# Copying both channels of a pair with one instruction in an im2col kernel

## The chip, the cores and the metric

The kernel runs on one core of a Trainium2 chip. The metric is the device time of one execution in microseconds (us). All executions quoted are fast (none took over 1.5% more than the fastest of its kernel), and every comparison of times is between runs of the same rounds on the same chip. Traces are single executions, and those of different groups of runs come from different chips. The profile comes from one execution of each kernel; its span (89.6 us here) is shorter than the device time (91.4 us for that execution).

## The reference

Each 3 x 3 window of a 32 x 32 image becomes a column. There are 16 x 64 images (fp32); each gives 9 planes of 30 x 30, one for each position (i, j) in the window, so the output has nine planes for each input image:

```python
# ... (cut: the loop over the batch b, which sets col_idx to 0)
for i in range(h_out):
    for j in range(w_out):
        patch = x[b, :, i:i + kernel_size, j:j + kernel_size].copy()
        cols[b, :, col_idx] = patch.ravel()
        col_idx += 1
```

No arithmetic is done. 4.19 MB are read from device memory (HBM) and 33.18 MB are written.

## The kernel before

Each of the 128 partitions holds eight images ("channels" below), treated in four pairs. A first load brings pair 0, a second one the other three. VectorE and ScalarE copy a pair's 18 planes from the input tile to an output tile, and one DMA stores the tile. There are two output tiles, so pair 2 must wait until the store of pair 0 has given its buffer back.

```python
in_pool = ctx.enter_context(tc.tile_pool(name="in_pool", bufs=1))
out_pool = ctx.enter_context(tc.tile_pool(name="out_pool", bufs=2))
# ... (cut)
first = load(0, 2 * H)
load(2 * H, CPP * H)

def planes(c, ki, kj, n, step):
    w = in_tile[:, c, ki : ki + HO, kj : kj + WO]
    part, row, col = [list(d) for d in w.ap]
    return bass.AP(w.tensor, w.offset, [part, [step, n], row, col])

for c in range(0, CPP, 2):
    out_tile = out_pool.tile([P, 2, KK, HO, WO], x.dtype, name="out_tile")
    for s in range(2):
        o = out_tile[:, s]
        nc.scalar.copy(out=o[:, K : 2 * K], in_=planes(c + s, 1, 0, K, 1))
        for ki in (0, 2):
            nc.vector.tensor_copy(
                out=o[:, ki * K : ki * K + 2], in_=planes(c + s, ki, 0, 2, 1)
            )
        # ... (cut: planes 2 and 8. For s == 0 one VectorE copy of both,
        #      for s == 1 plane 2 on VectorE and plane 8 on ScalarE)
    nc.sync.dma_start(
        out=out_v[:, c : c + 2].rearrange("p c n -> p (c n)"),
        in_=out_tile.rearrange("p c kk i j -> p (c kk i j)"),
    )
```

Of the kernel before, what the change touches and what calls it, by code (L numbers as in the profile page):

```python
# [1 line left out]

# [3 lines left out]


def _im2col(ctx, tc, x, K, out):


    nc = tc.nc
    P = nc.NUM_PARTITIONS

    B, C, H, W = x.shape
    HO = H - K + 1
    WO = W - K + 1
    KK = K * K
    assert out.shape == (B, C * KK, HO * WO)
    CPP = B * C // P
    assert CPP * P == B * C and C % CPP == 0 and CPP % 2 == 0 and K == 3  # L20

    x_v = x.rearrange("b (cp c2) h w -> (b cp) (c2 h w)", c2=CPP)
    out_v = out.rearrange("b (cp c2 kk) n -> (b cp) c2 (kk n)", c2=CPP, kk=KK)

    in_pool = ctx.enter_context(tc.tile_pool(name="in_pool", bufs=1))
    out_pool = ctx.enter_context(tc.tile_pool(name="out_pool", bufs=2))

    ctx.enter_context(tc.manual_schedule())

    in_tile = in_pool.tile([P, CPP, H, W], x.dtype, name="in_tile")  # L30
    in_flat = in_tile.rearrange("p c h w -> p (c h w)")

    def load(r0, r1):

        return nc.sync.dma_start(
            out=in_flat[:, r0 * W : r1 * W],
            in_=x_v[:, r0 * W : r1 * W],
        )

    first = load(0, 2 * H)  # L40
    load(2 * H, CPP * H)

    def planes(c, ki, kj, n, step):

        w = in_tile[:, c, ki : ki + HO, kj : kj + WO]
        part, row, col = [list(d) for d in w.ap]
        return bass.AP(w.tensor, w.offset, [part, [step, n], row, col])

    for c in range(0, CPP, 2):
        out_tile = out_pool.tile([P, 2, KK, HO, WO], x.dtype, name="out_tile")  # L50


        for s in range(2):
            o = out_tile[:, s]
            nc.scalar.copy(out=o[:, K : 2 * K], in_=planes(c + s, 1, 0, K, 1))  # L55
            for ki in (0, 2):
                nc.vector.tensor_copy(  # L57
                    out=o[:, ki * K : ki * K + 2], in_=planes(c + s, ki, 0, 2, 1)
                )
            if s == 0:  # L60
                nc.vector.tensor_copy(  # L61
                    out=o[:, 2:KK:6], in_=planes(c + s, 0, 2, 2, 2 * W)
                )
            else:
                nc.vector.tensor_copy(  # L65
                    out=o[:, 2], in_=in_tile[:, c + s, 0:HO, 2 : 2 + WO]
                )
                nc.scalar.copy(  # L68
                    out=o[:, 8], in_=in_tile[:, c + s, 2 : 2 + HO, 2 : 2 + WO]
                )  # L70
        nc.sync.dma_start(  # L71
            out=out_v[:, c : c + 2].rearrange("p c n -> p (c n)"),
            in_=out_tile.rearrange("p c kk i j -> p (c kk i j)"),
        )
    return first


def kernel(
    tc: tile.TileContext,
    x: bass.AP,  # L80
    kernel_size: bass.AP,
    out: bass.AP,
):
    with ExitStack() as ctx:
        first = _im2col(ctx, tc, x, int(kernel_size), out)


    tc.close()
    tc.compile()  # L89
    blocks = tc.nc.main_func.blocks  # L90
    load = first.ins
    home = next(b for b in blocks if any(i.name == load.name for i in b.instructions))
    home.instructions = [i for i in home.instructions if i.name != load.name]
    head = list(blocks[0].instructions)
    at = next(
        k
        for k, i in enumerate(head)
        if i.engine == load.engine and type(i).__name__ == "InstDrain"
    )
    head.insert(at, load)  # L100
    blocks[0].instructions = head


# [1 line left out]
_INS = ['x', 'kernel_size']  # L105
_OUTS = [((16, 576, 900), 'float32')]

_NUMBERS = {'kernel_size': 3}


# [26 lines left out]
```

## Time and profile before

| what | value |
|---|---|
| device time, median of 3 runs | 91.12 us (91.10 to 91.21) |
| profiled span | 89.6 us |
| VectorE / ScalarE busy | 25% / 27% of the span |
| DMA queue, share of 16 engines' span | 97.2% |
| first store issued | 10.69 us |

Read the engines' shares against the queue's share first. A queue at 97% leaves 3% to be won by work that feeds it, and only from stretches in which it stands idle. The groups by shape (busy us, mean ns of one | idle before, releasers) give the price of each kind of copy. L57 and L61 copy 1800 elements each by different patterns and take the same time (1092 and 1090 ns), so neither pattern is slower than the other:

```profile
L55 ACT COPY out_tile<-in_tile 128x2700 f32<-128x2700 f32 x8 | 19.2, 2443 | 31.7 <-DMA out_dram<-out_tile 27.1 <-DMA in_tile<-in_x_dram 4.5
L57 DVE COPY out_tile<-in_tile 128x1800 f32<-128x1800 f32 x16 | 16.8, 1092 | 33.7 <-DMA out_dram<-out_tile 27.1 <-DMA in_tile<-in_x_dram 6.6
L61 DVE COPY out_tile<-in_tile 128x1800 f32<-128x1800 f32 x4 | 4.4, 1090 | 0.0
L68 ACT COPY out_tile<-in_tile 128x900 f32<-128x900 f32 x4 | 3.8, 938 | 0.0
L65 DVE COPY out_tile<-in_tile 128x900 f32<-128x900 f32 x4 | 2.5, 620 | 0.0
```

### The profile page before, as it was taken

What the parts mean: (1) busy time and instruction counts of PE and PEld (TensorE: products, weight loads), DVE (VectorE), ACT (ScalarE), POOL (GpSimd) and SP (SyncE); (2) the same over time, 40 slices, a digit from 0 to 9 for tenths busy, and PEclk for the clock granted to TensorE, in tenths of its full rate; (3) what the DMA queues carried; (4) which work ended last, traced back from release to release, by engine and by line L of the source; (5) the groups of instructions that cost most, each with busy time, mean ns of one, the idle gap of its engine ahead of it and who ended that gap; (6) DMA issues with size and microseconds to landing.
All of it is one profiled execution on the core that took longest, in us unless ns stands there. A gap on an engine that the chain in (4) does not pass through costs nothing.

```text
span 89.6 us, 96 instructions
## 1 busy us (share of the span) xinstructions
DVE 22.6 (25%) x24; ACT 23.8 (27%) x13; POOL 0.2 (0%) x4
## 2 busy tenths in 40 slices
DVE  0079759900000099500000399100000000000000
ACT  5079759900000099500000399100000000000000
POOL 0000000000000000000000000000000000000000
DMA  5989899999999999947999999999999982999990
GB/s 128 505 384 494 362 463 463 463 463 463 463 463 463 463 463 463 434 174 318 463 463 463 463 463 463 463 463 463 463 463 463 463 347 116 463 463 463 463 463 0
DMA packets 864, 37.37 MB, mean 417 GB/s; under 512 B 96, under 2 KB 96, under 8 KB 96
## 3 DMA queue, kind: packets, MB, share of 16 engines
q1 hardware_dynamic: 864, 37.37, 97.2%
HBM read 4.19 MB, written 33.18 MB: 417 GB/s over the span
## 4 chain that ended last, share of the span: by engine, by line
DMA 49%; DVE 12%; DVEq 1%; issue 0%; SPq 0%
DMA out_dram<-out_tile 36%; DMA in_tile<-in_x_dram 13%; DVE out_tile L57 8%; DVE out_tile L61 2%; DVE out_tile L65 1%; DVEq L89 1%; DVEq L57 0%; SPq L71 0%
## 5 line engine op out<-in xcount | busy, mean ns | idle before, releaser
L55 ACT COPY out_tile<-in_tile 128x2700 f32<-128x2700 f32 x8 | 19.2, 2443 | 31.7 <-DMA out_dram<-out_tile 27.1
L57 DVE COPY out_tile<-in_tile 128x1800 f32<-128x1800 f32 x16 | 16.8, 1092 | 33.7 <-DMA out_dram<-out_tile 27.1
L61 DVE COPY out_tile<-in_tile 128x1800 f32<-128x1800 f32 x4 | 4.4, 1090 | 0.0
L68 ACT COPY out_tile<-in_tile 128x900 f32<-128x900 f32 x4 | 3.8, 938 | 0.0
L65 DVE COPY out_tile<-in_tile 128x900 f32<-128x900 f32 x4 | 2.5, 620 | 0.0
L55 ACT ACT_TABLE_LOAD x1 | 1.3, 1283 | 0.8 <-PEq L118 0.8
L118 POOL MEMSET const-bfloat16-1.0<- 128x1 bf16 x1 | 0.1, 101 | 0.0
L118 POOL MEMSET const-uint8-127<- 128x1 uint8 x1 | 0.1, 101 | 0.0
L118 POOL MEMSET const-float32-0.0<- 128x1 f32 x1 | 0.1, 98 | 0.2 <-issue 0.2
L118 POOL MEMSET const-float32-1.0<- 128x1 f32 x1 | 0.1, 98 | 0.0
## 6 DMA issues: line engine op xcount, KB each, us to landing
out_dram<-out_tile SPq DMA_DIRECT2D x4, 8100.0 KB, 32.4
in_tile<-in_x_dram SPq DMA_DIRECT2D x1, 3072.0 KB, 11.4
in_tile<-in_x_dram SPq DMA_DIRECT2D x1, 1024.0 KB, 4.9
```

What stands on the lines that cost most here:

```text
L55: nc.scalar.copy(out=o[:, K : 2 * K], in_=planes(c + s, 1, 0, K, 1))
L57: nc.vector.tensor_copy(out=o[:, ki * K : ki * K + 2], in_=planes(c + s, ki, 0, 2, 1))
L61: nc.vector.tensor_copy(out=o[:, 2:KK:6], in_=planes(c + s, 0, 2, 2, 2 * W))
L65: nc.vector.tensor_copy(out=o[:, 2], in_=in_tile[:, c + s, 0:HO, 2 : 2 + WO])
L68: nc.scalar.copy(out=o[:, 8], in_=in_tile[:, c + s, 2 : 2 + HO, 2 : 2 + WO])
L89: tc.compile()
L118: nc = _bacc.Bacc("TRN2", target_bir_lowering=False, num_devices=1)
```

## The change

The intent is fewer instructions for the same bytes: a source pattern with one more dimension, the channel, lets one copy cover both channels. VectorE goes from six copies per pair to three, ScalarE from three to two. Which planes each engine copies stays the same in number (11 and 7).

```diff
-    def planes(c, ki, kj, n, step):
+    def windows(c, n, ki, kj, m):
-        w = in_tile[:, c, ki : ki + HO, kj : kj + WO]
-        part, row, col = [list(d) for d in w.ap]
-        return bass.AP(w.tensor, w.offset, [part, [step, n], row, col])
+        w = in_tile[:, c : c + n, ki : ki + HO, kj : kj + WO]
+        part, chan, row, col = [list(d) for d in w.ap]
+        return bass.AP(w.tensor, w.offset, [part, chan, [1, m], row, col])
 ... (cut: the copies of before, shown above, go out)
+        for on_act, s, n, ki, kj, m in (
+            (True, 0, 2, 1, 0, K),
+            (False, 0, 2, 0, 0, K),
+            (False, 0, 2, 2, 0, 2),
+            (False, 0, 1, 2, 2, 1),
+            (True, 1, 1, 2, 2, 1),
+        ):
+            src = windows(c + s, n, ki, kj, m)
+            dst = out_tile[:, s : s + n, ki * K + kj : ki * K + kj + m]
+            if on_act:
+                nc.scalar.copy(out=dst, in_=src)
             else:
 ... (cut)
+                nc.vector.tensor_copy(out=dst, in_=src)
```

More of the change, by code (lines that the diff above doesn't have):

```diff
@@ L41, in _im2col @@
     load(2 * H, CPP * H)
-    def planes(c, ki, kj, n, step):
-        w = in_tile[:, c, ki : ki + HO, kj : kj + WO]
-        part, row, col = [list(d) for d in w.ap]
-        return bass.AP(w.tensor, w.offset, [part, [step, n], row, col])
+    def windows(c, n, ki, kj, m):
+        w = in_tile[:, c : c + n, ki : ki + HO, kj : kj + WO]
+        part, chan, row, col = [list(d) for d in w.ap]
+        return bass.AP(w.tensor, w.offset, [part, chan, [1, m], row, col])
     for c in range(0, CPP, 2):
         out_tile = out_pool.tile([P, 2, KK, HO, WO], x.dtype, name="out_tile")
-        for s in range(2):
-            o = out_tile[:, s]
-            nc.scalar.copy(out=o[:, K : 2 * K], in_=planes(c + s, 1, 0, K, 1))
-            for ki in (0, 2):
-                nc.vector.tensor_copy(
-                    out=o[:, ki * K : ki * K + 2], in_=planes(c + s, ki, 0, 2, 1)
-                )
-            if s == 0:
-                nc.vector.tensor_copy(
-                    out=o[:, 2:KK:6], in_=planes(c + s, 0, 2, 2, 2 * W)
-                )
-            else:
-                nc.vector.tensor_copy(
-                    out=o[:, 2], in_=in_tile[:, c + s, 0:HO, 2 : 2 + WO]
-                )
-                nc.scalar.copy(
-                    out=o[:, 8], in_=in_tile[:, c + s, 2 : 2 + HO, 2 : 2 + WO]
-                )
+        for on_act, s, n, ki, kj, m in (
[9 more added lines that the diff above has]
+                nc.scalar.copy(out=dst, in_=src)
+            else:
+                nc.vector.tensor_copy(out=dst, in_=src)
         nc.sync.dma_start(
```

## The prediction

Passages for which no trace or run of this case stands are cut from the text, and the cuts are marked. The forecast's sum is 91.12 − 0.06 = 91.06 us. Of the rates, 0.522 ns per element is VectorE's and 0.836 ScalarE's; that the new copies would run at them was an estimate. Rival 1 supposes that VectorE needs twice its measured time per element (1.044 ns) for the large copies, whose patterns have four dimensions (2 channels, 3 or 2 planes, 30 rows, 30 columns). Rival 3 supposes that they take a quarter longer (a guess, also the "small collision" of the range) because what one copy reads and writes lies farther apart: 4,096 and 32,400 bytes from channel to channel, where L57 has 4 and 3,600 from plane to plane.

> **What bounds the kernel now.** I read the page first, parts 1 and 3: which engine is busy, and how busy the transfer queue is.
>
> ```profile
> DVE 22.6 (25%) x24; ACT 23.8 (27%) x13; POOL 0.2 (0%) x4
> ...
> q1 hardware_dynamic: 864, 37.37, 97.2%
> ```
>
> VectorE and ScalarE each work for a quarter of the 89.6 us span; packets of the one DMA queue fill 97.2% of 16 engines' span. So the copies matter only where the queue would otherwise stand idle. The chain of waits, second, tells where the copies lie beside transfers (start, us, what):
>
> ```profile
> 0.79 11.40 DMA in_tile<-in_x_dram
> ...
> 17.33 0.55 DVE out_tile L65
> ...
> 17.95 32.59 DMA out_dram<-out_tile
> ...
> 50.65 1.10 DVE out_tile L57
> ```
>
> It needs care. It follows the last engine instruction, so it stops at 56.3 us, and it shows a copy of pair 3 waiting for a store to give its buffer back. The reader might take those copies (12% of the span) for critical. They are not: the store of pair 1 lands at 50.5, but the store of pair 2 was issued at 37.25 (timeline of the issuing queue) and stands behind it, so the transfers go on while pair 3 is built. Landings, from issue plus time to landing, are 31.4, 50.5, 69.7 and 88.8: even steps of 19.1 us, which is 8,294,400 bytes at 434 GB/s. Only the first pair's copies lie ahead of any store. The timeline shows that stage (start, length, engine, line):
>
> ```profile
> 4.93 4.79 ACT L55 COPY out_tile<-in_tile 128x2700 f32<-128x2700 f32 x2 [2.87 <-DMA in_tile<-in_x_dram]
> 4.93 2.10 DVE L57 COPY out_tile<-in_tile 128x1800 f32<-128x1800 f32 x2 [4.93 <-DMA in_tile<-in_x_dram]
> 6.96 1.09 DVE L61 COPY out_tile<-in_tile 128x1800 f32<-128x1800 f32 x1
> 7.96 2.10 DVE L57 COPY out_tile<-in_tile 128x1800 f32<-128x1800 f32 x2
> 9.63 0.94 ACT L68 COPY out_tile<-in_tile 128x900 f32<-128x900 f32 x1
> 9.97 0.62 DVE L65 COPY out_tile<-in_tile 128x900 f32<-128x900 f32 x1
> 10.69 7.60 SPq L71 DMA_DIRECT2D out_dram<-out_tile  x2
> ```
>
> ScalarE ends at 10.57, VectorE at 10.59; the first store is issued at 10.69. Is the queue idle then? Windows of 0.1 us, which book a packet where it starts (last two columns: DMA share, GB/s):
>
> ```profile
> 10.00:10.10 0.10, 0.10 (x2) 0.10 (x1) 0.00 (x0) 1.00 0.57 246
> ...
> 10.90:11.00 0.10, 0.00 (x0) 0.00 (x0) 0.00 (x0) 1.00 0.57 246
> ...
> 11.50:11.60 0.10, 0.00 (x0) 0.00 (x0) 0.00 (x0) 1.00 15.20 6480
> 11.60:11.70 0.10, 0.00 (x0) 0.00 (x0) 0.00 (x0) 1.00 7.60 3240
> ...
> 11.80:11.90 0.10, 0.00 (x0) 0.00 (x0) 0.00 (x0) 1.00 1.50 648
> ```
>
> The sixteen last packets of the second load (24,576 bytes, 0.912 us each in the trace's packet records) start between 10.0 and 11.0; by those records they end from 11.24 to 11.83, fifteen of them by 11.56. The first packets of the store start from 11.54 to 11.84. So the first store's packets start 0.85 us after its issue, just as the load runs out. Some engines stand idle for up to 0.3 us. The last one goes from its load packet to its store packet in 2 ns.
>
> [...] by the groups of instructions VectorE's 1800 elements take 1090 ns and 900 take 620, a slope of 470/900 = 0.522 ns per element[...]. In both large new copies the outermost dimension is the channel, count 2, on both sides. [...] (2443 − 938)/1800 = 0.836 ns per element, 186 ns fixed, and two copies in 4.79 us overlap by 0.096. [...]
>
> **The change part by part.** The change's title counts eleven instructions before; the page counts nine per pair (24 copies of VectorE and 12 of ScalarE in four pairs). VectorE has six copies before (five of 1800, one of 900) and three after (5400, 3600, 900); ScalarE three before (2700, 2700, 900) and two after (5400, 900). The two loads, the stores, the buffers and the elements per engine (9,900 and 6,300) stay as they are. Both channels of a pair arrive in one load, so one instruction over both waits for nothing new.
> - VectorE. Before: five steps of (9.97 − 4.93)/5 = 1.008 us, then 0.62: 5.66 us, ending at 10.59. One copy overlaps the next by 1.090 − 1.008 = 0.082. After: the large ones are 150 + 0.522 × 5400 = 2970 ns and 150 + 0.522 × 3600 = 2030 ns. 2.97 − 0.08 + 2.03 − 0.08 + 0.62 = 5.46 us, ending at 10.39. Saving 0.20 us.
> - ScalarE. Before 4.79 + 0.94 less 0.09: 5.64 us, ending at 10.57. After: 186 + 0.836 × 5400 = 4700 ns; 4.70 − 0.10 + 0.94 = 5.54 us, ending at 10.47. Saving 0.10 us.
> - ScalarE now ends last. Issue follows at 10.47 + 0.10 = 10.57, which is 0.12 us earlier, and the first store packets could start at 11.42.
>
> What is on the path: only this 0.12 us of pair 0. The load itself still ends from 11.24 to 11.83. Five engines gain the full 0.12, ten gain 0 to 0.12 and the last gains nothing. As the store ends when its slowest engine ends, and the sixteen land within 0.18 us of each other, I expect 0.00 to 0.10 off the end and choose 0.06: about half[...]. In the three other pairs, the 0.12 us falls into time in which a store is in flight, with slack of 31.4 − 18.0 = 13 us for pair 1, 13 for pair 2 (37.25 against 50.5) and 13 for pair 3 (56.4 against 69.7). It is worth nothing there. Sum: 91.12 − 0.06 = 91.06 us.
>
> **The rivals.**
> 1. [...] the two large copies would cost 0.15 + 1.044 × 5.4 = 5.79 and 3.91 us; pair 0 would end at 4.93 + 5.79 + 3.91 − 0.16 + 0.62 = 15.09, and the store start 4.5 us later, with the queue empty: 95.6 us, 5% slower. The other pairs' 13 us of slack would hide it. For it: before, no copy has more than three such dimensions in its recorded pattern. Against: [...] the record's patterns have room for four.
> 2. *A new wait between the engines.* ScalarE writes planes 3 to 5 of both channels, VectorE planes 0 to 2 and 6 to 7 around them. If the dependences were kept by enclosing ranges, one engine would wait for the other, and pair 0 would take 5.5 + 5.4 us rather than 5.66: again some 96 us. Against: L61 before writes planes 2 and 8 as one stepped pattern, which encloses planes 3 to 5 of the same channel. It started at 6.96, with no idle time, while ScalarE's copy of those planes ran until 7.38. So the dependences saw between the steps there; I do not know that they do for the larger patterns.
> 3. [...] A quarter more time would make VectorE's large copies 1.25 us longer and cost some 1.1 us (92.2). Against: L61 reads 256 and writes 21,600 bytes apart and takes 1090 ns like L57.
> 4. *The whole 0.12 us comes through*[...]: 91.0. In the extreme this is still 0.13%.
>
> **Range and chances.** The three runs before spread over 0.11 us. From 0.12 us gained and a run's scatter below, and a scatter and small collision above: 90.9 to 91.35. Faster by 2% would need 1.8 us, fifteen times what the copies can give on the path: 0.01. Rivals 1 and 2 get 4% each, rival 3 near 1%: slower 0.08. The rest, 0.91, is within 2%.
>
> **What would show it.** VectorE's forms: 128x5400 near 2970 ns, 128x3600 near 2030, 128x900 at 620; ScalarE's: 5400 near 4700. In pair 0 ScalarE ends last, near 10.47, and the store is issued near 10.57; its first packets start near 11.42 and its last first packet still near 11.84. Landings keep steps of 19.1 us. A 5400 copy near 5800 ns is rival 1; idle time of one engine until the other within a pair is rival 2; 3000 to 3800 ns is rival 3. I am wrong if the time leaves 90.9 to 91.35, or if the copies are as told and the end moves by more than the first store's issue does.

## The result, and the profile after

| | before | changed |
|---|---|---|
| median of six runs | 91.19 us (91.10 to 91.30) | 91.28 us (91.16 to 91.42) |
| ratio of changed to before | | 1.001, 95% interval 0.9996 to 1.0024 |

A ratio is the mean time of one kernel's fast runs over that of the other's of the same rounds, so not quite the ratio of the medians. The time before is here the median of six runs, three of them those of the section above.

From the page of the changed kernel, the engines and the queue:

```profile
DVE 21.8 (24%) x12; ACT 23.5 (26%) x9; POOL 0.2 (0%) x4
...
q1 hardware_dynamic: 864, 37.37, 97.1%
```

The groups by shape:

```profile
L63 ACT COPY out_tile<-in_tile 128x5400 f32<-128x5400 f32 x4 | 18.8, 4701 | 31.9 <-DMA out_dram<-out_tile 27.3 <-DMA in_tile<-in_x_dram 4.7
L65 DVE COPY out_tile<-in_tile 128x5400 f32<-128x5400 f32 x4 | 11.9, 2974 | 34.3 <-DMA out_dram<-out_tile 27.5 <-DMA in_tile<-in_x_dram 6.8
L65 DVE COPY out_tile<-in_tile 128x3600 f32<-128x3600 f32 x4 | 8.1, 2029 | 0.0
L63 ACT COPY out_tile<-in_tile 128x900 f32<-128x900 f32 x4 | 3.8, 938 | 0.0
L65 DVE COPY out_tile<-in_tile 128x900 f32<-128x900 f32 x4 | 2.5, 623 | 0.0
```

Half as many VectorE instructions save 0.8 us of its busy time in the whole kernel. The copies after the first of a pair have no idle time before them, so no engine waits for the other inside a pair. The timeline of the first pair (several copies of one line are merged under the shape of the first):

```profile
4.95 5.54 ACT L63 COPY out_tile<-in_tile 128x5400 f32<-128x5400 f32 x2 [2.88 <-DMA in_tile<-in_x_dram]
4.95 5.45 DVE L65 COPY out_tile<-in_tile 128x5400 f32<-128x5400 f32 x3 [4.95 <-DMA in_tile<-in_x_dram]
10.52 0.35 SPq L66 DMA_DIRECT2D out_dram<-out_tile  x1
```

VectorE ends at 10.40 and ScalarE at 10.49; the store is issued at 10.52, which is 0.17 us earlier than before. Here are the windows at the junction of load and store, a packet booked where it starts (last two columns: DMA share, GB/s):

```profile
11.30:11.40 0.10, 0.00 (x0) 0.00 (x0) 0.00 (x0) 1.00 4.59 1944
11.40:11.50 0.10, 0.00 (x0) 0.00 (x0) 0.00 (x0) 1.00 13.64 5832
11.50:11.60 0.10, 0.00 (x0) 0.00 (x0) 0.00 (x0) 1.00 4.52 1944
...
11.80:11.90 0.10, 0.00 (x0) 0.00 (x0) 0.00 (x0) 1.00 1.50 648
```

Set them beside those of before: the bulk of the first store packets moves forward, but one packet still starts between 11.8 and 11.9, as before. By its time it belongs to the DMA engine whose load ends last: the packet records of the trace (start, length and size of every DMA packet) carry no engine number, but that store packet starts within 2 ns of the end of the last load packet. By these records the last store packet lands at 88.30 us, before at 88.33.

### The profile page after: what moved, and what is told of

Same layout as the page of the kernel before. It is cut to its first block, busy times and chain, and to the rows that moved or that the text cites. A ratio compares the mean times of both kernels' runs of the same rounds, so it can differ in the third digit from the quotient of the medians.

```text
span 89.6 us, 80 instructions
## 1 busy us (share of the span) xinstructions
DVE 21.8 (24%) x12; ACT 23.5 (26%) x9; POOL 0.2 (0%) x4
## 4 chain that ended last, share of the span: by engine, by line
DMA 49%; ACT 11%; ACTq 1%; issue 0%
DMA out_dram<-out_tile 36%; DMA in_tile<-in_x_dram 13%; ACT out_tile L63 11%; ACTq L84 1%; ACTq L63 0%
## 5 line engine op out<-in xcount | busy, mean ns | idle before, releaser
L63 ACT COPY out_tile<-in_tile 128x5400 f32<-128x5400 f32 (+1 forms) x8 | 22.2, 2819 | 31.9 <-DMA out_dram<-out_tile 27.3
L65 DVE COPY out_tile<-in_tile 128x5400 f32<-128x5400 f32 (+2 forms) x12 | 21.8, 1875 | 34.3 <-DMA out_dram<-out_tile 27.5
```

Source lines behind the costliest of these rows:

```text
L63: nc.scalar.copy(out=dst, in_=src)
L65: nc.vector.tensor_copy(out=dst, in_=src)
```

## The experiments

All kernels gave correct results. Diffs are against the changed kernel. "Jobs" stands for the list of tuples (engine is ScalarE, first channel, channels, row, column, planes).

**Each engine's part alone.** `e5_scalar_part` keeps the old VectorE copies, `e6_vector_part` the old ScalarE copies.

```diff
 e5_scalar_part, jobs (the copy at row 0, column 2 of two planes has its old stepped pattern)
-            (False, 0, 2, 0, 0, K), (False, 0, 2, 2, 0, 2), (False, 0, 1, 2, 2, 1),
+            (False, 0, 1, 0, 0, 2), (False, 0, 1, 2, 0, 2), (False, 0, 1, 0, 2, 2),
+            (False, 1, 1, 0, 0, 2), (False, 1, 1, 2, 0, 2), (False, 1, 1, 0, 2, 1),
 e6_vector_part, jobs
-            (True, 0, 2, 1, 0, K),
+            (True, 0, 1, 1, 0, K), (True, 1, 1, 1, 0, K),
```

> ScalarE's part of the change alone (5400 and 900); VectorE keeps its six copies. Only the later engine of pair 0 counts: VectorE ends 5.66 us after the start of the copies and the first store is issued 5.76 us after it, as before (10.69 - 4.93), nothing gained. If shorter ScalarE work alone moved the issue, 5.57 as with both parts. Time 91.3, the same.

> VectorE's part alone (5400, 3600, 900); ScalarE keeps its three copies. ScalarE ends 5.64 us after the start of the copies. If the issue comes 0.03 us after ScalarE where it is last and 0.10 after VectorE where that is last, as the two traces so far suggest, the store is issued 5.67 us after the start: half of the change's 0.19 us from VectorE's part alone, of which 0.07 is the shorter way from ScalarE's end to the issue. If that way is 0.10 whichever engine is last, 5.74. Time 91.3, the same; the end of the last store follows the last load packet by 76.5 us in both runs.

Times: 91.20 us (ratio to before 0.9991, 0.9976 to 1.0006) and 91.30 us (0.9999, 0.9983 to 1.0016). From the start of the copies to the issue of the first store the traces give 5.75 us before, 5.75 with ScalarE's part, 5.66 with VectorE's part and 5.57 with both. So the later engine sets the issue, and the way from its end to the issue depends on which engine it is. The chain of waits shows where the difference lies. This is pair 1 before, VectorE last:

```profile
17.33 0.55 DVE out_tile L65
17.88 0.02 issue
17.90 0.02 SPq L71
17.92 0.03 issue
17.95 32.59 DMA out_dram<-out_tile
```

and here pair 1 of the changed kernel, ScalarE last:

```profile
12.26 5.55 ACT out_tile L63 x2
17.82 0.02 issue
17.84 32.70 DMA out_dram<-out_tile
```

With VectorE last there is one more step on the issuing queue (SPq L71, 0.02 us, and 0.03 us after it) before the store goes out. From the end of the last copy of pair 0 to the issue, both kernels' traces have 0.09 us with VectorE last and 0.03 with ScalarE last. Of the 0.18 us that the change gained on the issue, this step is 0.07; the rest is the shorter stage.

**Pair 0 made longer.** One more copy by VectorE of what it has just copied:

```diff
-        ):
+        ) + (((False, 0, 2, 0, 0, K),) if c == 0 else ()):
```

> One more 5400-element copy of VectorE in pair 0 alone (writes the same data again). Theory that only pair 0's copies are on the path: the first store is issued near 13.39 instead of 10.52, its first packets start near 14.24 on all sixteen engines together, and the time grows by 2.55 us to 93.8 (2.4 to 2.75). Rival, that the queue or later slack takes the delay up: under 92.0.

It took 93.86 us against 91.30 before (ratio 1.0282, 1.0267 to 1.0297). The store was issued at 13.29. By the packet records all sixteen first packets start between 14.14 and 14.29, so the whole load is long over, and the end moved by 2.6 us. Pair 0 is on the path, once its store is later than the load.

**Pairs 1 to 3 made longer.** The same copy twice more in each:

```diff
-        ):
+        ) + (((False, 0, 2, 0, 0, K),) * 2 if c > 0 else ()):
```

> Two more 5400-element copies of VectorE in each of pairs 1, 2 and 3: 5.8 us more per pair, 17.4 us in all. Slack theory: stores 1 to 3 are issued 5.7 us later, still behind a store in flight, and the time stays at 91.2 within 0.15. Rival, that buffers given back later or copies beside transfers cost time: 97 us if one pair's extra work shows, 108 if all do.

It took 91.29 us against 91.30 (ratio 1.0005, 0.9989 to 1.0022). The timeline shows that the extra work is there, pair 2 for example:

```profile
31.35 11.34 DVE L65 COPY out_tile<-in_tile 128x5400 f32<-128x5400 f32 x5 [7.94 <-DMA out_dram<-out_tile]
```

5.9 us more per pair disappear in the wait for a buffer, which shrinks from 13.8 to 7.9 us. The 17.7 us more of VectorE's work in all, beside running transfers, did not slow them by anything the times show (ratio 1.0005).

**Pair 2 made longer than its slack.** Five more copies in pair 2 alone:

```diff
-        ):
+        ) + (((False, 0, 2, 0, 0, K),) * 5 if c == 4 else ()):
```

> Five more 5400-element copies of VectorE in pair 2 alone: 14.4 us more, which is more than the slack of pair 2 by my count (its store is issued near 37.06 and its first packets go at 49.79, 0.85 us after the latest issue that costs nothing: slack 11.9 us). Expected: issue near 51.5, first packets near 52.35, end 2.55 us later: 93.85 us (93.6 to 94.1). If the slack is larger or smaller than that, the time is off by the difference; if VectorE beside transfers costs nothing at all, 91.3.

It took 94.03 us, two runs, against 91.35 (ratio 1.0297, 1.0276 to 1.0318). The first packets of that store start at 52.72 on average instead of 49.79, 2.92 us later. The expectation was 0.3 us short on the issue (51.83 instead of 51.5). The chain of waits shows why: each repeat starts 0.03 us after the end of the one before it, which writes the same planes, so it takes 3.01 us from start to start and not 2.89 (2.97 less the overlap of 0.08 that the prediction read between other copies):

```profile
39.76 2.98 DVE out_tile L65
42.75 0.02 issue
42.77 2.98 DVE out_tile L65
```

The slack is 11.8 us, against 11.9 in the expectation (first packets at 49.79 on average in the changed kernel, less 0.89 from issue to first packet in this run, less the issue at 37.07). That is over a microsecond less than the 13 us of the prediction, which counted up to the landing of the store ahead (50.5) and had not taken off the time from issue to first packet.

**Other shapes of copy, where they cost nothing.** In pair 1 the 5400-element copy is two copies of one channel's three planes; in pair 3 VectorE and ScalarE copy columns of the window (planes 0, 3 and 6, and so on).

```diff
+        if c == 2:
+            jobs[1:2] = [(False, 0, 1, 0, 0, K), (False, 1, 1, 0, 0, K)]
+        if c == 6:      # for kj = 2 on ScalarE, kj = 0 and 1 on VectorE, s = 0 and 1:
+            op(out=out_tile[:, s, kj : KK : K], in_=[part, [W, K], row, col])   # abridged
```

> The changed kernel with other shapes of copy in pairs 1 and 3 only, where I hold 13 us of slack. Pair 1: the 5400-element copy of VectorE as two copies of one channel's three planes (128x2700; source count 3 outermost, destination one run). [...] 0.15 + 1.044 x 2.7 = 2.97 us each. [...] Pair 3: VectorE copies columns of the window, three planes with stride in source and destination[...]. Time: slack theory 91.2 us within 0.2 although pair 1 gets 2.9 us longer and pair 3 longer too; if the copies of every pair count, 94 us or more.

The 2.97 us is an estimate at 1.044 ns per element, twice the 0.522 of the kernel before; at 0.522 itself it would be 1.56 us. The author expected 2.97 for the rows and 1.56 for the columns.

The time was 91.26 us against 91.30, two runs (ratio 0.9998, 0.9978 to 1.0018), although VectorE worked 8.3 us on pair 1 and 7.8 us on pair 3. The groups by shape (L72 are the columns, L82 the rows):

```profile
L72 DVE COPY out_tile<-in_tile 128x2700 f32<-128x2700 f32 x4 | 7.8, 2022 | 13.7 <-DMA out_dram<-out_tile 13.7
...
L82 DVE COPY out_tile<-in_tile 128x2700 f32<-128x2700 f32 x2 | 5.8, 2962 | 1.8 <-DMA in_tile<-in_x_dram 1.8
```

Rows: 2962 ns, which less the 150 ns of the prediction is 1.04 ns per element, twice the 0.522. Columns: 2022 ns or 0.69 ns per element, which neither estimate gives: three planes took as long as the 3600 elements of four (2028 ns in the same run). What in VectorE sets these rates is not shown. What the traces do show is that the change's 5400-element copy, the same rows of three planes with the channel (count 2) as the outermost dimension, takes 2974 ns or 0.52 ns per element, half of what the copies of one channel's rows need per element.

**A store issued early.** If the idle time before the first store were worth anything, an earlier store should win it. Pair 0 is copied by channel, with a store for each:

```diff
+        if c == 0:
+            for s in range(2):
+                # the old copies of channel s, then
+                nc.sync.dma_start(
+                    out=out_v[:, s],
+                    in_=out_tile[:, s].rearrange("p kk i j -> p (kk i j)"),
+                )
+            continue
```

> Pair 0 with copies by channel and a store of its own for each channel, so that the first store is issued near 8.1 instead of 10.52; pairs 1 to 3 as changed. Theory that the engine whose load ends last sets the end: no engine idles between load and store, the last store packet to start first still starts near 11.82, and the time stays within 0.1 of the changed kernel (91.2). Rival, that the end follows the mean engine or the first store's issue: 0.1 to 0.3 us faster than the changed kernel, at most 91.1. [...]

It took 92.68 us against 91.30 (ratio 1.0152, 1.0137 to 1.0167): slower by 1.4 us, which neither theory allowed. The DMA issues (KB each, us to landing) point at another place, the second load. The changed kernel, then this run:

```profile
in_tile<-in_x_dram SPq DMA_DIRECT2D x1, 3072.0 KB, 11.4
```

```profile
in_tile<-in_x_dram SPq DMA_DIRECT2D x1, 3072.0 KB, 12.7
```

By the packet records, a packet of this load takes 0.912 us in the kernels of before and after (128 of 128 and 127 of 128), but here 33 of those that start after 8 us take 0.947 to 1.814 us, the first such packet starting at 8.6. Three runs separate the split from the early issue. `e8_split_late` stores in two halves after all copies of pair 0. `e9_early_1us_later` and `e10_early_2us_later` are the early store with one and two more 1800-element copies ahead of the first half's store:

```diff
+                ) + (((False, 1, 0, 0, 2),) * 1 if s == 0 else ()):     # * 2 in the other
```

> Pair 0's store in two halves as in the early-store run, but both issued after all of pair 0's copies, near 10.5 and 10.9. If the 1.4 us of the early-store run came from the split (one more store, shorter packets), this takes 92.7 us too. If they came from issuing a store while the second load was still under way, this takes 91.3 within 0.15, and its load packets all take 0.912 us.

> The early-store run with one more 1800-element copy ahead of the first half store: issued near 9.05 instead of 8.03. If a store slows the load packets that are under way from about 0.9 us after its issue, only the last packet of each engine (0.912 us before, starting from 9.9) is slowed: loads end about 0.6 us later than in the changed kernel, 91.9 us (91.6 to 92.2). If the split costs it, 92.7 as before.

> The same with two more such copies: first half store issued near 10.05. Slowing from about 0.9 us after issue meets only the tails of the last load packets (they end from 11.2 to 11.8): at most 0.15 us later than the changed kernel, 91.3 to 91.45. If the split costs it, 92.7.

| run | first store issued | packets of load 2 over 0.93 us, after 8 us | last packet of load 2 ends | time, ratio to before |
|---|---|---|---|---|
| e4_early_store | 8.03 | 33 of 128 | 13.17 | 92.68, 1.0152 |
| e9_early_1us_later | 9.05 | 16 | 12.25 | 91.75, 1.0047 (1.0031 to 1.0064) |
| e10_early_2us_later | 10.19 | 0 | 11.69 | 91.41, 1.0011 (0.9996 to 1.0026) |
| e8_split_late | 10.41 | 0 | 11.77 | 91.44, 1.0012 (0.9996 to 1.0029) |

The split costs nothing that the interval of e8 can tell from zero; by its packet records the last store packet lands 76.59 us after the load's last packet, 0.1 us more than with one store (table below). A store issued early enough, here at 8.03 and 9.05 us, slows the last load packets (to 1.81 us at most in e4, from 0.912), although its own packets start only as the engines' loads end (from 12.04 us in e4, where the first engine's load ends at 12.03). In e4 48 load packets had still to start at the issue, and 33 were slow; in e9 32 had still to start, and 16 were slow. Shared out evenly over sixteen engines (the records name none), that is three per engine with the last two slow in nearly all, and two with the last one slow. The packets that ended within 1.5 us of the issue kept their 0.91 us, so the slowing sets in later than the 0.9 us of the expectation; in the changed kernel all load packets have ended 1.3 us after the issue. The lost time is not made up later: in e4 and e9 the last store packet lands 76.54 us after the last load packet. What in the DMA engines makes those packets slow is not settled by these runs.

**What sets the end.** From the packet records of single executions with one store per pair and no pair delayed beyond its slack (e2 and e7 are left out):

| run | first store issued | last packet of load 2 ends | last store packet lands | difference of the last two |
|---|---|---|---|---|
| before | 10.69 | 11.83 | 88.33 | 76.49 |
| changed | 10.52 | 11.82 | 88.30 | 76.48 |
| e1_forms | 10.43 | 11.73 | 88.22 | 76.49 |
| e3_delay_rest | 10.34 | 11.69 | 88.18 | 76.50 |
| e5_scalar_part | 10.51 | 11.62 | 88.13 | 76.51 |
| e6_vector_part | 10.54 | 11.79 | 88.28 | 76.49 |

Issues spread over 0.35 us and landings over 0.20; the last column spreads over 0.03. The end follows the engine whose load ends last, not the issue. e5 and the changed kernel make it plainest: issued within 0.02 us of each other, they end 0.17 us apart, as their loads do (0.20). The first two columns give the reason. A store's first packets start 0.85 us after its issue at the earliest (before and changed alike), and in all six runs the last load packet ends 1.11 to 1.35 us after the issue, so the last engine never waits for the issue.

The other engines did gain. The sixteen last store packets (2.39 us each and landing this close together, so taken as one of each engine) land at 88.23 us on average before and at 88.08 in the changed kernel, 0.14 us earlier, while the last of them moves by 0.03; their spread grows from 0.18 to 0.32 us. (These are single traces, and the loads' own last packets end 0.06 us earlier in the mean.) What the other fifteen engines won did not help the last one. In e4 the same shows at a larger size: loads that end from 12.03 to 13.17 us are followed by landings from 88.75 to 89.70, and the last landing still comes 76.54 us after the last load packet.

## Why the prediction was right

The prediction said 91.06 us and "within 2%", and the range 90.9 to 91.35 holds the measured 91.28. Point by point:

- **The bound.** That the copies matter only in pair 0 was right: nearly 18 us more VectorE work in the other pairs left the time at 91.29 us, 2.9 us more in pair 0 cost 2.6. But "only this 0.12 us of pair 0" was not on the path of the last engine either: before the change, its load ended 1.15 us after the issue, and a store's first packets need 0.85, so pair 0 had 0.3 us of slack of its own. The slack of 13 us was about one too large, as the delayed pair 2 showed.
- **The costs.** VectorE's copies were to take 2970 and 2030 ns and took 2974 and 2029; ScalarE's 4700 and took 4701. Stage lengths of 5.46 and 5.54 us came out as 5.45 and 5.54.
- **The issue.** It was to be 0.12 us earlier and was 0.17; counted from the start of the copies, 0.18. The mis-sized term is "Issue follows at 10.47 + 0.10": the 0.10 was VectorE's way to the issue (0.09 when not rounded), and with ScalarE last it is 0.03. The runs with one engine's part alone show it.
- **The end.** "I expect 0.00 to 0.10 off the end and choose 0.06: about half" was too generous. By the trace the last landing moved by 0.03 us, and reckoned from the last load packet by 0.01. The step that failed is the "half", an estimate for which no trace gave a reason: the engines that started earlier landed earlier, 0.14 us in the mean, and the last engine, which never waited for the store's issue, had nothing of it. The text had seen that engine and hedged; the table of six runs shows that it alone counts. Single runs of the changed kernel spread over 0.26 us, so the difference between 0.06 and 0.01 shows in the traces only, not in the times.
- **What was luck.** The measured median is 0.09 us above that of before, not 0.06 below, and is still in the range; two of the six runs (91.38 and 91.42) are above it. The kernel before had medians from 91.12 to 91.35 us in the different rounds, more than the change that was forecast. "Within 2%" did not depend on luck, the place in so narrow a range did.
- **The rivals.** Twice the time per element: 2974 ns, no. It was a sound fear, though: a single channel's three planes do take that long (2962 ns for half the elements). A wait between the engines: no idle time inside a pair. Slower copies because of what lies farther apart: 4 ns on 2970 at most. The whole gain coming through: no; the end does not follow the issue.

What the prediction had not seen is a danger on the other side. A store issued much earlier, at 8.0 instead of 10.5, made the kernel 1.5% slower, as it met the load.

## What to carry to other kernels

Before shortening work that feeds a DMA queue, look at what the queue still has to do when that work ends: here the last engine was still loading (until 11.82 us) when the first store's packets started (11.37), so 0.17 us gained before it bought nothing that the times show. Work out the slack of each later stage, up to the time when its transfer could first start and less the time from issue to first packet, and hide there whatever is slow. When VectorE copies rows of three planes, try a dimension like the channel (count 2) outermost: here that took 0.52 ns per element against 1.04 for one channel alone. Each instruction saved was worth only 0.07 to 0.10 us of its engine's time here.
